# FFN 2 of a hybrid encoder block: two plain feature tiles of gate and up become an eleventh seven-product unit

## The chip, the cores and the metric

One core of one Trainium2 chip runs the whole kernel. The metric is the device time of one execution in microseconds (us), the median of several runs. Engines are named as in the profile: PE (matrix products), PEld (its weight loads), DVE (vector engine), ACT (scalar engine), POOL, and SP, which here issues most transfers. Each engine works off its own queue in the order in which the built program stands, and waits there for what another engine has to deliver.

## What is computed

The reference is one encoder layer on 512 tokens of width 1024: a half-step feed-forward (FFN 1), a mixing block (recurrent branch and attention, joined by a product with W_out), and a second half-step feed-forward (FFN 2). The change is in FFN 2:

```
def _rmsnorm(x, g):
    y = xf * lax.rsqrt(jnp.mean(xf * xf, axis=-1, keepdims=True) + EPS)
    return (y * g.astype(jnp.float32)).astype(x.dtype)

def _swiglu(h, w_gu, w_down):
    g, u = jnp.split(h @ w_gu, 2, axis=-1)
    return (jax.nn.silu(g) * u) @ w_down

x = x + (sigmoid(gA)*A + sigmoid(gB)*B) @ W_out
x = x + 1/2 * SwiGLU_2(RMSNorm(x))
```

D_FF is 2816, so gate and up have 22 feature tiles of 128 each.

## The kernel before, in words

Activations are held transposed: a tile has 128 features on the partitions and all 512 tokens along the row. Every product of float32 numbers is made of three products of rounded halves: an operand is cut into a high part (xh, wh; cast by ACT, L138) and a low part (xl, wl; the rest, subtracted by DVE, L141), and the PE adds high by high, high by low and low by high (`mm3`, L164).

**The step ahead of FFN 2** is the product with W_out (L988 to L1000). For each of 8 output tiles m the PE does 24 matmuls; then DVE adds the residual (L994), ACT makes xh (L187), a square (L196) and a scaled copy xg (L541), and DVE makes xl (L188) and adds the square to `ssum` (L197). From m = 4 on, `Forms.tile` makes four sums and differences of quarters of x ("forms" s1, s2, s4, s3, L238 to L264) for the pair (m - 4, m); `cut` splits them into high and low (L266), two pairs at a time, behind m = 5 and behind m = 7.

**A plain feature tile** (L417 to L428) takes two chunks, gate and up, of 24 matmuls of 512 tokens each (`feat_chunk`, L169; the weights come through `load_w`, L152). FFN 2 has `NPLAIN[1]` = 2 of these in front. Behind the first chunk stands `rstd` (L201): the PE transposes `ssum` (L211), DVE sums it (L212), ACT takes the root, DVE the reciprocal, the PE transposes it back (L219), and ACT writes the row of 1/rms that scales gate and up afterwards.

**A unit of seven products** (`strassen`, L273) makes two feature tiles of gate and of up at once by a Strassen-like scheme: gate and up on one side, the two halves of the tokens on the other, the inner dimension in two halves. Each `product` (L279) is 24 matmuls of 256 tokens. Per unit four blocks of 512 KB of weights are loaded: `a_` and `b_` into the buffers `wraw` (3 of them), `d` and `c` into buffers `pair` (4, which also hold the residual tiles). Four times two blocks are added on DVE (`after_sum`, L324, done at L323), and seven operands are split (`operand`, L292), into buffers wh and wl, of which there are 4 each: the eighth split waits until the fourth product is done, and so on. In the first unit the products are, in the order of the code, a11 on the operand `a_`, a12 on `c` (`gate1`, L333), then s1, s2, s4 and s3 on sums or on `b_`; the seventh (a22) is done inside the next unit. a11 uses xh and xl of the tiles 0 to 3, a12 of the tiles 4 to 7. The second product's result is scaled by 1/rms in `gate` (L298).

**What sets the order.** No order is written out: the framework's scheduler puts each engine's instructions in a row when the program is built. Splits of weights and sums of blocks are marked `tc.high_priority()` (L160, L294, L325), so the scheduler places them as early as it can.

Of the kernel before, what the change touches and what calls it, by code (L numbers as in the profile page):

```python
# [9 lines left out]
F32 = mybir.dt.float32  # L10
# [6 lines left out]
P = 128  # L17
T = 512
D = 1024
KT = D // P  # L20
DFF = 2816
FT = DFF // P
# [20 lines left out]
NLEAD = 6  # L43


NPLAIN = 4, 2

DTAIL = 3

# [2 lines left out]
AHEAD = 4  # L52
# [32 lines left out]
def block_kernel(ctx: ExitStack, tc, a, out):  # L85
# [3 lines left out]
    xpool = ctx.enter_context(tc.tile_pool(name="xpool", bufs=1))  # L89
# [11 lines left out]
    def nm(s):  # L101
        uid[0] += 1
        return f"{s}_{uid[0]}"
# [12 lines left out]
    def aux_t():  # L116
        return aux.tile([P, T], F32, tag="aux", name=nm("aux"))
# [4 lines left out]
    xd = dram.tile([KT, P, T], F32, name="xd")  # L122
# [75 lines left out]

        return xh, xl, ssum, one, square

    def rstd(ssum, lead=False):  # L201

        pc = aux_t()
        vx = tiny.tile([P, NCB], F32, tag="vx", name=nm("vx"))
        if lead:
            for j in range(NCB):
                nc.tensor.matmul(pc[:, j : j + 1], ssum[:, j * P : (j + 1) * P], ones[:, 0:1], start=True, stop=True)
            nc.vector.tensor_scalar(vx, pc[:, 0:NCB], 1.0 / D, EPS, ALU.mult, ALU.add)
        else:
            for j in range(NCB):  # L210
                nc.tensor.transpose(pc[:, j * P : (j + 1) * P], ssum[:, j * P : (j + 1) * P], ident)  # L211
            nc.vector.reduce_sum(vx, pc.rearrange("p (j f) -> p j f", j=NCB), axis=AX.X)  # L212
            nc.vector.tensor_scalar(vx, vx, 1.0 / D, EPS, ALU.mult, ALU.add)
        rcol = tiny.tile([P, NCB], F32, tag="rcol", name=nm("rcol"))
        nc.scalar.activation(rcol, vx, AF.Sqrt)
        nc.vector.reciprocal(rcol, rcol)
        ps = aux_t()
        for j in range(NCB):
            nc.tensor.transpose(ps[:, j * P : (j + 1) * P], rcol[:, j : j + 1].to_broadcast([P, P]), ident)  # L219
        r = xpool.tile([P, T], F32, tag="rstd", name=nm("rstd"))  # L220
        nc.scalar.activation(r, ps, AF.Copy)
        return r, rcol, vx

# [46 lines left out]

        return S, raw, cut

    def strassen(src, units, A, r, hs, ahead):  # L273

        half = T // 2
        prev = {}
        view = lambda t: t.rearrange("p (m t) -> p m t", m=2)

        def product(ps, w, form, first, last):  # L279
            H, L = w  # L280
            for m in range(2):
                o = ps[:, m * half : (m + 1) * half]
                for k in range(4):
                    c = slice((m * 4 + k) * P, (m * 4 + k + 1) * P)
                    xh_, xl_ = A[form][k]


                    for w_, x_ in ((H, xh_), (H, xl_), (L, xh_)):
                        nc.tensor.matmul(o, w_[:, c], x_, start=first and m + k == 0 and w_ is H and x_ is xh_,  # L289
                                         stop=m + k == 4 and w_ is L, skip_group_check=True)  # L290

        def operand(raw):  # L292
            w = hl_t()
            with tc.high_priority():  # L294
                split(raw, *w)
            return w

        def gate(t, tok):  # L298
            rr = r[:, tok].unsqueeze(1).to_broadcast([P, 2, half])
            s_ = big_t(n="s")  # L300
            nc.vector.tensor_tensor(view(s_), view(t), rr, ALU.mult)
            nc.scalar.activation(s_, s_, AF.Silu)
            return s_

        def put(u, s_, t, tok):
            for m in range(2):
                c = slice(m * half, (m + 1) * half)
                mark["h"] = nc.vector.tensor_tensor(hs[u * 2 + m][:, tok], s_[:, c], t[:, c], ALU.mult)

        def last_product(p):  # L310
            product(p["Z"], p["w"](), "a22", False, True)
            put(p["u"], gate(p["Z"], slice(half, T)), p["u7"], slice(half, T))

        for u in range(units):
            a_, b_ = raw_t(), raw_t()
            d = pair_t().rearrange("p a b -> p (a b)")
            c = pair_t().rearrange("p a b -> p (a b)")

            for t, i in ((a_, 0), (d, 1), (b_, 3), (c, 2)):
                nc.sync.dma_start(t, src[u, i])  # L320

            def add(t, o, i):
                nc.vector.tensor_tensor(t, t, o, ALU.add)  # L323
            def after_sum(t, o, i, add=add):  # L324
                with tc.high_priority():  # L325
                    add(t, o, i)
                return operand(t)

            Z, X, Y = acc_t(), acc_t(), aux_t()
            hs += [big_t(n="h") for _ in range(2)]  # L330
            last = u == units - 1

            def gate1():  # L333
                product(Y, w_c, "a12", True, True)
                nc.vector.tensor_tensor(p1, p1, Y, ALU.add)
                return gate(p1, slice(0, half))

            product(Z, operand(a_), "a11", True, False)
            p1 = big_t(n="p1")
            nc.scalar.activation(p1, Z, AF.Copy)  # L340
            w_c = operand(c)
            if not last:
                s1 = gate1()
            product(X, after_sum(a_, d, 1), "s1", True, False)
            p5 = big_t(n="p5")
            nc.scalar.activation(p5, X, AF.Copy)
            if prev:
                last_product(prev)
            product(Z, after_sum(a_, b_, 3), "s2", False, False)
            u2 = big_t(n="u2")  # L350
            nc.scalar.activation(u2, Z, AF.Copy)
            product(X, operand(b_), "s4", False, True)
            nc.vector.tensor_tensor(u2, u2, X, ALU.add)
            product(Z, after_sum(b_, d, 1), "s3", False, False)
            nc.vector.tensor_tensor(p5, p5, Z, ALU.add)
            if last:
                ahead()
                s1 = gate1()
            put(len(hs) // 2 - 1, s1, u2, slice(0, half))
            prev = dict(u=len(hs) // 2 - 1, Z=Z, u7=p5, w=lambda a_=a_, c=c, f=after_sum: f(a_, c, 2))  # L360
        last_product(prev)

    def ffn(wgu, ws, wd, xh, xl, S, ssum, plain, res, emit_out, lead=None, end=None):
        hs = []
        r = None
        pre = {}
        if lead is not None:
# [5 lines left out]
            for k in range(KT):  # L373
                lead[0](k)
                if k in LEAD_W:
                    n = LEAD_W[k]
                    o = (k % 4) * P
# [19 lines left out]
                w = [wts[i][k // 4] for i in range(NLEAD)]  # L397
                lead[2](k)
                if k == KT - 1:
                    r = rstd(ssum, True)[0]  # L400
# [16 lines left out]
        for m in range(plain):  # L417
            pg = chunk(2 * m)
            if r is None:
                r = rstd(ssum)[0]  # L420
            pu = chunk(2 * m + 1)
            g = big_t(n="g")
# [8 lines left out]
        A = {"a11": quarter(0, slice(0, half)), "a12": quarter(4, slice(0, half)),  # L431
             "a22": quarter(4, slice(half, T)), **S}
# [5 lines left out]
        def ahead(n):  # L438
            while len(cuts) < min(n, len(order)):
                qk = order[len(cuts)]  # L440
                cuts[qk] = big_t(F32R, n="hh"), big_t(F32R, n="hl")
                split(hs[qk[1]], *cuts[qk])

        strassen(ws, (FT - plain) // 2, A, r, hs, lambda: ahead(AHEAD))
        for q in range(2):
            outs = range(q * 4, q * 4 + 4)
            for i in range(2):
# [36 lines left out]
        i, x, k0 = 3, xres[KT - 1], FT - EHALF  # L484
        for k in range(FT - 2 * DTAIL, k0):
            put_in(i, k, k0 - 1)
        t, o, p2 = big_t(n="dn"), big_t(n="o"), aux_t()[:, :half]
# [40 lines left out]
    xh, xl, ssum, one, square = make_xg(C_G1, "a")  # L528
# [32 lines left out]
    forms = Forms(C_G1)  # L561
# [10 lines left out]
    def out1(m, ps):  # L572
# [6 lines left out]

    ffn(a["w1gu"], a["w1s"], a["w1d"], xh, xl, forms.S, ssum, NPLAIN[0], lambda m: a["x"][m], out1,  # L580
        (lead, one, lead_step, lambda: (forms.finish(), forms.finish())))
    xh, xl, ssum = nxt["v"][:3]
# [152 lines left out]
    A = [None] * KT  # L735
# [225 lines left out]
    for w, fn, scale in ((0, AF.Gelu_apprx_tanh, 1.0), (1, AF.Tanh, 0.5)):  # L961
        for fs in (range(0, 4), range(4, 8)):
            for f, t in gates(w, fs, fn, scale):
                until("lru", lambda: A[f] is not None)
                if w == 0:
                    o = big_t(n="A")
# [20 lines left out]
    forms = Forms(C_G2)  # L987
# [13 lines left out]
    xh, xl, ssum = nxt["v"][:3]  # L1001


    def out2(m, ps):
# [1 line left out]
        nc.vector.tensor_tensor(o, ps, xres[m], ALU.add)  # L1006
        nc.sync.dma_start(out[m], o)

    ffn(a["w2gu"], a["w2s"], a["w2d"], xh, xl, forms.S, ssum, NPLAIN[1], lambda m: xd[m], out2,
        end=lambda tok, o: nc.sync.dma_start(out[KT - 1][:, tok], o[:, tok]))  # L1010


def layouts(inp):

    f = lambda n: np.asarray(inp[n])
    con = np.ascontiguousarray
    o = {}
# [7 lines left out]
    for i in (1, 2):  # L1025
        w = f(f"w_ffn{i}_gu")[0]
        g, u = feat(w[:, :DFF]), feat(w[:, DFF:])
        n = NPLAIN[i - 1]
        o[f"w{i}gu"] = con(np.stack([g, u], 1)[:n]).reshape(2 * n, P, D)

        b = np.stack([g, u], 0)[:, n:].reshape(2, (FT - n) // 2, 2, P, 2, D // 2)
        o[f"w{i}s"] = con(b.transpose(1, 4, 0, 3, 2, 5)).reshape((FT - n) // 2, 4, P, D)
        d = f(f"w_ffn{i}_down")[0].reshape(FT // 2, 2, P, 2, T)
        o[f"w{i}d"] = con(d.transpose(3, 0, 2, 1, 4)).reshape(2, FT // 2, P, 2 * T)
    w = f("w_in")[0].reshape(D, 7, D)
# [49 lines left out]
```

## Time and profile before

| what | value |
|---|---|
| median of 3 runs | 1127.6 us (1127.58 to 1127.77) |
| the profiled execution, its own time | 1127.92 us |
| its span, first to last instruction | 1125.7 us |
| PE busy | 1114.5 us (99%) |
| PEld busy | 983.4 us (87%) |
| DVE busy | 834.9 us (74%) |
| ACT busy | 592.9 us (53%) |
| POOL busy | 52.3 us (5%) |
| chain of work that ended last | PE 96%, DVE 2%, issue 1%, ACT 1% |
| granted TensorE clock | 1.00 |

The span is the time from the first to the last instruction on the core; the execution's own time has 2.2 us more around it. Matmuls overlap in the pipeline, so the duration that the profile gives for one is longer than the distance from one start to the next; the distance is what counts for a sum. In the chain the lengths are these distances already added up.

### The profile page before, as it was taken

The numbers are of one execution on the slowest core, as the hardware profiler recorded it, in microseconds if no ns is written. First come the engines' busy times: TensorE is split into PE (matmuls) and PEld (weight loads), VectorE is DVE, ScalarE is ACT, GpSimd is POOL, SyncE is SP. The second block draws the span as 40 slices with busy tenths as digits, with TensorE's granted clock in tenths as the row PEclk, the third lists the DMA queues.
The fourth block names the chain that finished last, engine by engine and source line by source line (L and its number), as shares of the span: only waits on it lengthen the run. The fifth ranks groups of instructions, "written<-read, shape, count | busy, mean of one in ns | idle before, by whom it ended". The sixth has DMA issues, their size and how long they took to land.

```text
span 1125.7 us, 17414 instructions
## 1 busy us (share of the span) xinstructions
PE 1114.5 (99%) x6867; PEld 983.4 (87%) x6867; DVE 834.9 (74%) x1294; ACT 592.9 (53%) x897; POOL 52.3 (5%) x116
## 2 busy tenths in 40 slices
PE   9999999999999999999999999999999999999998
PEld 8899999988888777777888888888999999998887
DVE  7888888893736865899655877659688888894552
ACT  8554554563533668687464445446445445464330
POOL 0000000000000341120110000000000000000000
PEclk9999999999999999999999999999999999999999
DMA  7242333443423686573443342355134233252421
GB/s 265 93 127 80 114 112 95 132 134 98 143 80 103 164 231 174 151 193 94 135 147 103 94 124 64 105 180 183 57 95 118 90 112 114 94 169 94 131 75 38
DMA packets 46770, 138.04 MB, mean 123 GB/s; under 512 B 7008, under 2 KB 10592, under 8 KB 46688
## 3 DMA queue, kind: packets, MB, share of 16 engines
q1 hardware_dynamic: 39744, 118.31, 33.8%
q0 software_dynamic: 6368, 18.36, 5.9%
q8 instruction: 54, 0.88, 0.3%
q10 hardware_dynamic: 576, 0.26, 0.1%
q14 instruction: 28, 0.23, 0.1%
HBM read 120.12 MB, written 8.39 MB: 114 GB/s over the span
## 4 chain that ended last, share of the span: by engine, by line
PE 96%; DVE 2%; issue 1%; ACT 1%; DVEq 0%; ACTq 0%
PE acc L289 29%; PE acc L165 11%; PE acc L166 11%; PE acc L167 11%; PE aux L289 5%; PE aux L167 4%; PE aux L165 4%; PE aux L166 4%; PE acc L761 3%; PE acc L763 3%; PE acc L762 3%; PE aux L883 1%; PE aux L895 1%; PE aux L675 1%; PE aux L854 1%
## 5 line engine op out<-in xcount | busy, mean ns | idle before, releaser
L138 ACT ACTIVATE wh<-wraw 128x1024 fp32r<-128x1024 f32 (+3 forms) x242 | 239.8, 993 | 327.5 <-PE acc L289 95.9
L141 DVE TENSOR_TENSOR wl<-wraw,wh 128x1024 fp32r<-128x1024 f32 (+3 forms) x254 | 289.5, 1142 | 143.4 <-ACT wh L138 140.1
L289 PE MATMUL acc<-s,wh 128*128 128x256 f32 x1216 | 220.5, 283 | 0.0
L289 PEld LDWEIGHTS acc<-s,wh 128*128 128x128 f32 x1216 | 189.7, 192 | 0.0
L289 PE MATMUL acc<-s,wl 128*128 128x256 f32 x608 | 172.1, 283 | 0.0
L165 PE MATMUL acc<-xh,wh 128*128 128x512 f32 x304 | 120.4, 396 | 0.0
L167 PE MATMUL acc<-xh,wl 128*128 128x512 f32 x304 | 118.9, 391 | 0.0
L166 PE MATMUL acc<-xl,wh 128*128 128x512 f32 x304 | 118.8, 391 | 0.0
L289 PEld LDWEIGHTS acc<-s,wl 128*128 128x128 f32 x608 | 116.8, 192 | 0.0
L289 PE MATMUL acc<-xh,wl 128*128 128x256 f32 x304 | 86.0, 283 | 0.0
L289 PE MATMUL acc<-xl,wh 128*128 128x256 f32 x304 | 86.0, 283 | 0.0
L289 PE MATMUL acc<-xh,wh 128*128 128x256 f32 x304 | 86.0, 283 | 0.0
L761 PE MATMUL acc<-wh,xh 128*128 128x512 f32 x192 | 75.8, 396 | 1.9 <-DVE v L785 1.4
L762 PE MATMUL acc<-wh,xl 128*128 128x512 f32 x192 | 75.1, 391 | 0.0
L763 PE MATMUL acc<-wl,xh 128*128 128x512 f32 x192 | 75.0, 391 | 0.0
L323 DVE TENSOR_TENSOR wraw<-wraw,pair 128x1024 f32<-128x1024 f32 x57 | 69.5, 1220 | 0.8
L165 PE MATMUL aux<-hh,wh 128*128 128x512 f32 (+1 forms) x181 | 69.9, 386 | 0.0
L166 PE MATMUL aux<-hl,wh 128*128 128x512 f32 (+1 forms) x181 | 69.9, 386 | 0.0
L167 PE MATMUL aux<-hh,wl 128*128 128x512 f32 (+1 forms) x181 | 69.9, 386 | 0.0
L167 PE MATMUL acc<-hh,wl 128*128 128x512 f32 (+1 forms) x176 | 67.9, 386 | 0.0
L166 PE MATMUL acc<-hl,wh 128*128 128x512 f32 (+1 forms) x176 | 67.9, 386 | 0.0
L165 PE MATMUL acc<-hh,wh 128*128 128x512 f32 (+1 forms) x176 | 67.9, 386 | 0.0
(212 smaller groups left out, 2206.8 us busy)
## 6 DMA issues: line engine op xcount, KB each, us to landing
wraw<-wqkv SPq DMA_DIRECT2D x24, 512.0 KB, 4.5
wraw<-wg SPq DMA_DIRECT2D x24, 512.0 KB, 3.6
wraw<-w1d SPq DMA_DIRECT2D x22, 512.0 KB, 3.6
wraw<-w2d SPq DMA_DIRECT2D x22, 512.0 KB, 3.6
pair<-w2s SPq DMA_DIRECT2D x20, 512.0 KB, 3.6
wraw<-w2s SPq DMA_DIRECT2D x20, 512.0 KB, 3.6
wraw<-w1s SPq DMA_DIRECT2D x18, 512.0 KB, 3.6
pair<-w1s SPq DMA_DIRECT2D x18, 512.0 KB, 3.7
```

Source lines behind the costliest of these rows:

```text
L138: nc.scalar.activation(H, raw, AF.Copy)
L141: nc.vector.tensor_tensor(L, raw, H.bitcast(F32), ALU.subtract)
L165: nc.tensor.matmul(ps, wh, xh, start=first, stop=False, skip_group_check=skip)
L166: nc.tensor.matmul(ps, wh, xl, start=False, stop=False, skip_group_check=skip)
L167: mark["mm"] = nc.tensor.matmul(ps, wl, xh, start=False, stop=last, skip_group_check=skip)
L289: nc.tensor.matmul(o, w_[:, c], x_, start=first and m + k == 0 and w_ is H and x_ is xh_, stop=m + k == 4 and w_ is L, skip_group_check=True)
L323: nc.vector.tensor_tensor(t, t, o, ALU.add)
L675: prev, mm = mm, nc.tensor.matmul(ps[d][b], W[w][o, c], X[x][o], start=x == 1, stop=w + x == 0)
L761: nc.tensor.matmul(pss[j], xh[kk][:, tj], H[:, s], start=kk == 0, stop=False)
L762: nc.tensor.matmul(pss[j], xl[kk][:, tj], H[:, s], start=False, stop=False)
L763: mark["mm"] = nc.tensor.matmul(pss[j], xh[kk][:, tj], L[:, s], start=False, stop=kk == KT - 1)
L854: mm = hold(nc.tensor.matmul(ps[hp][:, i * 256 : (i + 1) * 256], q_[o, n * P : (n + 1) * P], keys(k_[o]), start=k_ is kl, stop=q_ is ql))
```

## The change

FFN 2 has no plain tile: `NPLAIN` is `4, 0`, so all 22 feature tiles go through 11 units instead of 2 plain tiles and 10 units. As `rstd` stood behind the first plain chunk, it is now called inside the first unit, behind its second product (a12), and writes into a tile that is allocated ahead of the units. The weights of the two tiles move from the array of plain chunks to that of the units; their bytes stay the same.

```diff
-NPLAIN = 4, 2
+NPLAIN = 4, 0
...
-    def rstd(ssum, lead=False):
+    def rstd(ssum, lead=False, r=None):
...
-        r = xpool.tile([P, T], F32, tag="rstd", name=nm("rstd"))
+        if r is None:
+            r = xpool.tile([P, T], F32, tag="rstd", name=nm("rstd"))
...
-    def strassen(src, units, A, r, hs, ahead):
+    def strassen(src, units, A, r, hs, ahead, late=None):
...
             def gate1():
                 product(Y, w_c, "a12", True, True)
+                if u == 0 and late is not None:
+                    late()
                 nc.vector.tensor_tensor(p1, p1, Y, ALU.add)
                 return gate(p1, slice(0, half))
...
-        strassen(ws, (FT - plain) // 2, A, r, hs, lambda: ahead(AHEAD))
+        if r is None:
+            r = xpool.tile([P, T], F32, tag="rstd", name=nm("rstd"))
+            late = lambda: rstd(ssum, False, r)
+        else:
+            late = None
+        strassen(ws, (FT - plain) // 2, A, r, hs, lambda: ahead(AHEAD), late)
...
-    ffn(a["w2gu"], a["w2s"], a["w2d"], xh, xl, forms.S, ssum, NPLAIN[1], lambda m: xd[m], out2,
+    ffn(None, a["w2s"], a["w2d"], xh, xl, forms.S, ssum, NPLAIN[1], lambda m: xd[m], out2,
```

The order of the instructions changes only from the end of the W_out product on. In the rows below a tile's name is followed by its numbers.

**DVE, behind the last W_out tile (m = 7).** Here `acc_1414` is that tile's result, `xl_1359` the low part of x tile 7, `ssum_1360` the sum of squares. Before:

```order
L242 TENSOR_TENSOR s1_1410_7711<-xg_1409_7709,xg_1373_7517 128x256
L240 SCALAR_TENSOR_TENSOR s2_1411_7713<-s1_1410_7711,xg_1373_7517 128x256
L240 SCALAR_TENSOR_TENSOR s4_1412_7715<-s2_1411_7713,xg_1409_7709 128x256
L242 TENSOR_TENSOR s3_1413_7717<-xg_1373_7517 128x256
L994 SCALAR_TENSOR_TENSOR pair_1339_7380<-acc_1414_7720,pair_1339_7380 128x512
L141 TENSOR_TENSOR wl_1451_7900<-wraw_1449_7898,wh_1450_7899 128x1024
L188 SCALAR_TENSOR_TENSOR xl_1359_7428<-pair_1339_7380,small_78,xh_1358_7427 128x512
L197 TENSOR_TENSOR ssum_1360_7429<-ssum_1360_7429,xsq_1418_7754 128x512
```

And in the change, where `wraw_1429` holds a_ and the sums made of it, `wraw_1430` b_, `pair_1432` c and `pair_1431` d of the first unit:

```order
L243 TENSOR_TENSOR s1_1410_7711<-xg_1409_7709,xg_1373_7517 128x256
L1002 SCALAR_TENSOR_TENSOR pair_1339_7380<-acc_1414_7720,pair_1339_7380 128x512
L141 TENSOR_TENSOR wl_1452_7906<-wraw_1429_7781,wh_1451_7905 128x1024
L241 SCALAR_TENSOR_TENSOR s2_1411_7713<-s1_1410_7711,xg_1373_7517 128x256
L324 TENSOR_TENSOR wraw_1429_7781<-wraw_1429_7781,pair_1432_7784 128x1024
L141 TENSOR_TENSOR wl_1455_7936<-wraw_1430_7782,wh_1454_7935 128x1024
L241 SCALAR_TENSOR_TENSOR s4_1412_7715<-s2_1411_7713,xg_1409_7709 128x256
L324 TENSOR_TENSOR wraw_1430_7782<-wraw_1430_7782,pair_1431_7783 128x1024
L243 TENSOR_TENSOR s3_1413_7717<-xg_1373_7517 128x256
L188 SCALAR_TENSOR_TENSOR xl_1359_7428<-pair_1339_7380,small_78,xh_1358_7427 128x512
L197 TENSOR_TENSOR ssum_1360_7429<-ssum_1360_7429,xsq_1418_7754 128x512
```

Between the residual add of m = 7 and its xl stood one split of weights; now there are two splits, two sums of blocks and three forms.

**PE, where xl of x tile 7 is first used.** Before, it is the last k of the first plain chunk (`acc_1428`), with the transposes of `ssum` behind it:

```order
L165 MATMUL acc_1428_7780<-xh_1356_7425,wh_1430_7782 128x512
L166 MATMUL acc_1428_7780<-xl_1357_7426,wh_1430_7782 128x512
L167 MATMUL acc_1428_7780<-xh_1356_7425,wl_1431_7783 128x512
L165 MATMUL acc_1428_7780<-xh_1358_7427,wh_1430_7782 128x512
L166 MATMUL acc_1428_7780<-xl_1359_7428,wh_1430_7782 128x512
L167 MATMUL acc_1428_7780<-xh_1358_7427,wl_1431_7783 128x512
L211 MATMUL aux_1432_7811<-ident_83,ssum_1360_7429 128x128 x4
```

In the change it is inside the second product of the first unit (a12, `aux_1435`), of which ten matmuls stand ahead of these six of s1 (`acc_1434`), and fourteen from the xl row on:

```order
L290 MATMUL aux_1435_7791<-xh_1358_7427,wh_1441_7824 128x256
L290 MATMUL acc_1434_7790<-s1_1396_7654,wh_1448_7874 128x256
L290 MATMUL acc_1434_7790<-s1_1397_7655,wh_1448_7874 128x256
L290 MATMUL acc_1434_7790<-s1_1396_7654,wl_1449_7875 128x256
L290 MATMUL acc_1434_7790<-s1_1396_7654,wh_1448_7874 128x256
L290 MATMUL acc_1434_7790<-s1_1397_7655,wh_1448_7874 128x256
L290 MATMUL acc_1434_7790<-s1_1396_7654,wl_1449_7875 128x256
L290 MATMUL aux_1435_7791<-xl_1359_7428,wh_1441_7824 128x256
L290 MATMUL aux_1435_7791<-xh_1358_7427,wl_1442_7825 128x256
```

The first use of xl of tile 7 moved from the 23rd matmul of 512 tokens behind W_out to the 41st of 256; the transposes of `ssum` and the 18 other matmuls of s1 follow behind a12.

**PE, behind the product s1 of the first unit.** Before, s2 of the same unit (`acc_1459`) follows s1:

```order
L289 MATMUL acc_1460_7943<-s1_1420_7764,wh_1470_8010 128x256
L289 MATMUL acc_1460_7943<-s1_1421_7765,wh_1470_8010 128x256
L289 MATMUL acc_1460_7943<-s1_1420_7764,wl_1471_8011 128x256
L289 MATMUL acc_1459_7942<-s2_1398_7658,wh_1473_8041 128x256
L289 MATMUL acc_1459_7942<-s2_1399_7659,wh_1473_8041 128x256
```

In the change, seven matmuls of a11 of the second unit (`acc_1462`, with its split operand `wh_1467` and `wl_1468`) stand between s1 and s2 (`acc_1433`):

```order
L290 MATMUL acc_1434_7790<-s1_1420_7764,wl_1449_7875 128x256
L290 MATMUL acc_1462_8004<-xh_1344_7413,wh_1467_8009 128x256
L290 MATMUL acc_1462_8004<-xl_1345_7414,wh_1467_8009 128x256
L290 MATMUL acc_1462_8004<-xh_1344_7413,wl_1468_8010 128x256
L290 MATMUL acc_1462_8004<-xh_1346_7415,wh_1467_8009 128x256
L290 MATMUL acc_1462_8004<-xl_1347_7416,wh_1467_8009 128x256
L290 MATMUL acc_1462_8004<-xh_1346_7415,wl_1468_8010 128x256
L290 MATMUL acc_1462_8004<-xh_1348_7417,wh_1467_8009 128x256
L290 MATMUL acc_1433_7789<-s2_1398_7658,wh_1451_7905 128x256
```

The splits go through the four buffers in the order a_, c, s1, s2, s4, s3 of the first unit and then a_ of the second, so `wh_1467` takes the buffer of `wh_1448`, the operand of s1.

## Rows read from the trace of the kernel before

**Rows 1.** The page, busy time, share of the span and count by engine.

```profile
PE 1114.5 (99%) x6867; PEld 983.4 (87%) x6867; DVE 834.9 (74%) x1294; ACT 592.9 (53%) x897; POOL 52.3 (5%) x116
```

**Rows 2.** PE's longest wait in the span: total us, times, longest us.

```profile
PE acc L761 <- DVE v L785: 1.4, 1, 1.4
```

**Rows 3.** PE's order of time, W_out's end and the units' start: start, us.

```profile
777.61 0.39 PE L167 MATMUL acc<-yh,wl 128*128 128x512 f32 x1
777.84 0.39 PE L165 MATMUL acc<-xh,wh 128*128 128x512 f32 x1
...
800.54 0.28 PE L289 MATMUL acc<-xh,wh 128*128 128x256 f32 x1
800.66 0.28 PE L289 MATMUL acc<-xl,wh 128*128 128x256 f32 x1
```

**Rows 4.** The chain that ended last, same place: start, us, what.

```profile
783.45 0.44 PE aux L211 x4
...
790.49 0.44 PE aux L219 x4
...
820.86 2.88 PE aux L289 x24
...
841.02 2.88 PE aux L289 x24
```

**Rows 5.** Windows, units 3 to 10: us, then busy by engine, PEclk, DMA.

```profile
842.00:1005.00 163.00, 163.00 (x1349) 162.51 (x1349) 140.83 (x166) 84.72 (x105) 0.00 (x0) 1.00 0.38 117
```

**Rows 6.** DVE in order of time: start, us, instruction [idle before <- releaser].

```profile
761.72 0.69 DVE L994 SCALAR_TENSOR_TENSOR pair<-acc,pair 128x512 f32<-128x512 f32 x1 [2.08 <-PE acc L167]
...
768.07 1.23 DVE L141 TENSOR_TENSOR wl<-wraw,wh 128x1024 fp32r<-128x1024 f32 x1 [0.23 <-ACT wh L138]
...
777.14 0.41 DVE L242 TENSOR_TENSOR s<-xg,xg 128x256 f32<-128x256 f32 x1
777.59 0.88 DVE L240 SCALAR_TENSOR_TENSOR s<-s,xg 128x256 f32<-128x256 f32 x2
...
778.73 0.68 DVE L994 SCALAR_TENSOR_TENSOR pair<-acc,pair 128x512 f32<-128x512 f32 x1
779.33 1.21 DVE L141 TENSOR_TENSOR wl<-wraw,wh 128x1024 fp32r<-128x1024 f32 x1
780.46 0.75 DVE L188 SCALAR_TENSOR_TENSOR xl<-pair,small,xh 128x512 fp32r<-128x512 f32 x1
781.12 0.68 DVE L197 TENSOR_TENSOR ssum<-ssum,xsq 128x512 f32<-128x512 f32 x1
781.73 0.42 DVE L242 TENSOR_TENSOR s<-xg,xg 128x256 f32<-128x256 f32 x1
782.06 0.42 DVE L242 TENSOR_TENSOR s<-xg 128x256 f32<-128x256 f32 x1
...
786.72 1.22 DVE L323 TENSOR_TENSOR wraw<-wraw,pair 128x1024 f32<-128x1024 f32 x1
787.86 0.68 DVE L141 TENSOR_TENSOR s<-s,s 128x512 fp32r<-128x512 f32 x1
```

**Rows 7.** ACT and DVE in order of time: the split of a unit's operand.

```profile
800.57 1.06 ACT L138 ACTIVATE wh<-wraw 128x1024 fp32r<-128x1024 f32 x1 [3.85 <-PE acc L166]
...
801.66 1.23 DVE L141 TENSOR_TENSOR wl<-wraw,wh 128x1024 fp32r<-128x1024 f32 x1 [0.16 <-ACT wh L138]
```

**Rows 8.** SP in order of time: when block c of the first unit is issued.

```profile
759.14 0.33 SPq L320 DMA_DIRECT2D pair<-w2s  x1
```

**Rows 9.** Issues by line, 735 to 810 us: count, KB, median us to landing.

```profile
pair<-w2s SPq DMA_DIRECT2D x6, 512.0 KB, 4.3
```

**Rows 10.** PE in order of time, the kernel's first microseconds.

```profile
1.06 3.78 PE L131 MATMUL aux<-ones 128*128 128x128 f32 x16 [1.06 <-DVE pol L600]
4.69 1.65 PE L402 MATMUL acc<-xh,wh 128*128 128x512 f32 x3
6.13 0.93 PE L402 MATMUL aux<-xh,wh 128*128 128x512 f32 x3
```

More of the change, by code (lines that the diff above doesn't have):

```diff
@@ L1028, in layouts @@
         n = NPLAIN[i - 1]
-        o[f"w{i}gu"] = con(np.stack([g, u], 1)[:n]).reshape(2 * n, P, D)
+        if n:
+            o[f"w{i}gu"] = con(np.stack([g, u], 1)[:n]).reshape(2 * n, P, D)
         b = np.stack([g, u], 0)[:, n:].reshape(2, (FT - n) // 2, 2, P, 2, D // 2)
```

## Prediction, made before the changed kernel ran

> **What bounds the kernel now.** I read the page first: PE is busy for 99% of the span [rows 1], so time is saved by taking matmuls away and lost wherever PE is made to wait. Then the list of PE's waits: the longest single one is 1.4 us, in the attention part [rows 2], and none lies in FFN 2. Then the chain and PE's order of time at the place of the change. W_out's last matmul starts at 777.61 and the first plain chunk's at 777.84, with no gap; the first unit begins at 800.54 [rows 3]. From there the chain is PE alone, unit behind unit: the same product, a12, of units 2 and 3 stands at 820.86 and 841.02 [rows 4], so a unit takes 20.16 us, 0.120 us for each of its 168 matmuls. Last I read DVE at W_out's end, since DVE feeds PE there. It waits for W_out's result of m = 4 at 761.72, having idled 2.08 us, but adds the residual of m = 7 only at 778.73 [rows 6], some 0.7 us after that result could be had (three chunks of 5.44 us later than 761.72 is 778.04). So DVE is already a little late before the change, and what is put in its queue there counts.
>
> **Matmuls.** Removed: four chunks of 24 matmuls of 512. The stretch 777.84 to 800.54 is 22.70 us and holds them and two groups of transposes of 0.44 us [rows 3, 4], so they take 21.82 us, 0.227 each. Added: one unit, 20.16 us. The transposes stay. Saving: **1.7 us**. The Trainium skill, page "TensorE: Matmul & The Clock Gate", section "Wait — 56ns, not 53.3ns?", puts the distance of matmuls at columns over 2.4 GHz plus about 2.5 ns; by that, 96 of 512 less 168 of 256 would save 2.4 us, an estimate. The rows have 13 ns over the columns' own time in both sizes, and they decide.
>
> **DVE at W_out's end, first stall.** Between the residual add of m = 4 and xl of m = 7, DVE's queue before holds four splits of weights; in the change it holds five, and all four sums of the first unit's blocks; the forms and cuts ahead of that xl are as many as before. A split's subtract holds DVE for 1.13 us (779.33 to 780.46), a sum for 1.14 (786.72 to 787.86) [rows 6]. Added: 4 x 1.14 + 1.13 = 5.7 us. Some of it fills gaps: 0.23 us ahead of the subtract at 768.07, about as much ahead of the residual of m = 5, and 0.12 in front of each form that needs the one just made (777.14 to 777.59 is 0.45, where independent forms stand 0.33 apart, 781.73 to 782.06) [rows 6]; with four of the latter, 0.9 us. So xl of m = 7 starts not at 780.46 but 4.8 us later, at **785.2**, and is there at 786.0 (0.75 us) [rows 6]. The bounds are 786.2, if no gap is filled, and about 784.2, if twice as much is; I take the middle, because the gaps are rows.
>
> PE meanwhile runs a11 from 777.84, 24 x 0.12 = 2.9 us, ten matmuls of a12 (1.2) and the six of s1 that stand ahead of the xl row (0.7), and is at that row at 782.65. It waits until 786.0: **3.3 us** lost (2.4 to 4.3 by the bounds). Before, the same row stood 22 x 0.227 = 5.0 us behind 777.84, at 782.8, and xl was there at 781.2.
>
> **Second stall.** The rest of a12 (14), the transposes and the 18 other matmuls of s1 take 1.7 + 0.4 + 2.2 = 4.3 us, to 790.3. The squares' sum follows xl on DVE by 0.7 us [rows 6], in time for the transposes. Then come the seven matmuls of the second unit's a11. Their operand takes the buffer of s1's, so its cast can't start before s1's last matmul is through. What such a split costs from the moment that PE releases it: ACT casts for 1.06 us from 800.57, and DVE's subtract starts 0.03 us after that and lasts 1.23 [rows 7]. PE waits some 1.2 us for the cast (matmul's end included), does two matmuls, 0.24 us, and waits for the subtract for another 1.0 us: **2.2 us** lost. It is 1.2 at least, when the subtract is hidden somehow. Who waits for PE here is s2, whose operands have long been there; it follows undisturbed.
>
> **1/rms and the transfers.** `rstd`'s own work is the same, in another place. Behind xl, at 785.9, DVE has `ssum`, five forms and two cuts ahead of its reduction (0.60 or 0.33 each [rows 6], to 789.1), then the reduction, two splits, two cuts and a sum ahead of the small scaling; as the second of these splits ends only at 792.7 (above), that scaling comes at about 794.4, and root and reciprocal, tiny ones, at about 795.2. PE has been held until 792.75, does five more matmuls of a11, all of s2 and one more, and is at the transposes of L219 at 796.4. So 1/rms is covered by 1.2 us; without that cover PE would wait for it, and then `gate`, which is needed only for h. The two table loads of ACT stand in both orders. On SP the first unit's blocks take the places of the plain chunks; c, the latest of them, is issued as before at 759.14 [rows 8], takes some 4.3 us [rows 9], and is cast at about 767. Nothing else waits on SP there. In the later units DVE is busy for 140.8 of 163 us and PE for all of it [rows 5]; one more such unit brings no wait.
>
> **Sum.** -1.7 + 3.3 + 2.2 = **+3.8 us**. The profiled execution would go from 1127.9 to 1131.7; the median shown is 0.3 us lower, so I forecast **1131.4**.
>
> **Rivals.** A measurement of this kernel can tell about 0.2%, 2.3 us, from no change: same is 1125.3 to 1129.9.
>
> *xl is in time* (not slower). If xl of m = 7 starts by 781.9, the first stall is gone, and what is left is -1.7 + 2.2: 1128.1. It decides at DVE's queue between 779 and 785: two sums, two splits and three forms would have to be done by W_out's end. Against it: the splits wait for PE (the one of b_ until a11 is done, as it takes that buffer), and DVE is late already [rows 6]. 7%.
>
> *Neither stall*, the plain reading of the change as a saving of matmuls: 1125.9. For it speaks that PE never waits in the ten units of before [rows 5]; against it, that each of those starts with its operands made long ahead. 5%.
>
> *The clock falls behind the first stall* (slower still). No row of before has PE idle for over 1.4 us [rows 2], and the granted clock is 1.00 throughout, so what 3.3 us do is not shown. The nearest rows are the kernel's start: 16 warm-up matmuls take 3.78 us, the first ones of 512 stand some 0.6 us apart and the next group under 0.3 [rows 10]; some of that is waiting for weights. Were all of 1.06 to 6.13 at the 1.2 GHz level, that costs half of 5.1 us, so 2.5 us here too: 1133.9. The Trainium skill, same page, section "HAM oscillation — how this bites in real kernels", has idle gaps of PE throw the clock back to half, so that the next work starts cold; no run here shows that so far. 13%.
>
> *The lateness lasts*, another microsecond or more where the second unit's first operands are made, because DVE is behind with everything: 1133 to 1136. 7%.
>
> **The numbers.** The forecast has 68%: by the bounds of its two stalls (2.4 + 1.2 to 4.3 + 2.2) it lies between 1129.5 and 1132.4. With the clock's case the range goes to 1134.0; below, 1129.4 leaves out xl in time and no stall. Left out are some 14 to 18%. Slower: 68 + 13 + 7 = 88%, less 1 for the lower edge of the forecast; same: 7 + 5 - 1 + 1 = 12%; faster: 1%, if the whole saving is had and a little more.
>
> **What would show it.** In the new profile: PE's waits have two new entries of over 1 us, one for xl on DVE (about 3.3 us, at some 786) and one for the cast and the subtract of a split at some 790 to 793; xl of m = 7 starts near 785.2 on DVE; all units behind that run at 20.16 us without a gap; the granted clock stays 1.00. The prediction is wrong if PE runs through a12 without a wait, if a wait of over 1 us stands at L219 or in a later unit, or if matmuls behind the stall stand 0.24 us apart.

## The result, and the profile after

The changed kernel took 1132.47 us in the median of five runs (1132.33 to 1133.38), the kernel before 1127.69 us on the same chip (1127.58 to 1127.88): ratio 1.0044, interval 1.0030 to 1.0057, so slower by 4.8 us where 3.8 were forecast. The profiled execution took 1133.38 us (span 1131.2) at a mean granted clock of 0.998; the four others took 1132.33 to 1132.80 at 1.000. Run again on another chip (experiment e9_change_again, below) it had a median of 1133.72 us. Where that spread comes from is a part of the explanation.

The page of the changed kernel, busy time by engine, against [rows 1]; PE has 72 matmuls more, 168 of 256 for 96 of 512:

```profile
PE 1114.8 (99%) x6939; PEld 986.5 (87%) x6939; DVE 843.5 (75%) x1306; ACT 598.1 (53%) x903; POOL 52.2 (5%) x116
```

Its list of PE's waits (total us, times, longest us), the three entries that the list of before does not have; there the longest was 1.4 us [rows 2]:

```profile
PE aux L290 <- DVE xl L188: 3.3, 1, 3.3
...
PE acc L290 <- ACT wh L138: 1.1, 1, 1.1
...
PE acc L290 <- DVE wl L141: 0.8, 1, 0.8
```

DVE of the changed kernel in order of time, from the residual add of m = 4 and then from that of m = 7 on, against [rows 6]:

```profile
761.30 0.69 DVE L1002 SCALAR_TENSOR_TENSOR pair<-acc,pair 128x512 f32<-128x512 f32 x1 [2.08 <-PE acc L167]
...
764.02 1.22 DVE L324 TENSOR_TENSOR wraw<-wraw,pair 128x1024 f32<-128x1024 f32 x1
...
778.68 0.68 DVE L1002 SCALAR_TENSOR_TENSOR pair<-acc,pair 128x512 f32<-128x512 f32 x1
779.28 1.21 DVE L141 TENSOR_TENSOR wl<-wraw,wh 128x1024 fp32r<-128x1024 f32 x1
780.41 0.41 DVE L241 SCALAR_TENSOR_TENSOR s<-s,xg 128x256 f32<-128x256 f32 x1
780.75 1.22 DVE L324 TENSOR_TENSOR wraw<-wraw,pair 128x1024 f32<-128x1024 f32 x1
781.88 1.22 DVE L141 TENSOR_TENSOR wl<-wraw,wh 128x1024 fp32r<-128x1024 f32 x1
783.02 0.41 DVE L241 SCALAR_TENSOR_TENSOR s<-s,xg 128x256 f32<-128x256 f32 x1
783.35 1.22 DVE L324 TENSOR_TENSOR wraw<-wraw,pair 128x1024 f32<-128x1024 f32 x1
784.49 0.41 DVE L243 TENSOR_TENSOR s<-xg 128x256 f32<-128x256 f32 x1
784.83 0.74 DVE L188 SCALAR_TENSOR_TENSOR xl<-pair,small,xh 128x512 fp32r<-128x512 f32 x1
...
792.73 1.23 DVE L141 TENSOR_TENSOR wl<-wraw,wh 128x1024 fp32r<-128x1024 f32 x1 [0.74 <-ACT wh L138]
...
796.28 0.17 DVE L216 RECIPROCAL rcol<-rcol 128x4 f32<-128x4 f32 x1
```

DVE never idles from 778.68 to 785.6: two splits, two sums and three forms stand between the residual and xl, which starts 6.15 us behind the residual add instead of 1.73. On DVE the order changes earlier than "from the end of the W_out product on", as it is told above: the first sum of blocks stands at 764.02, behind xl of m = 4, and a second one at 775.34. PE's own order does change only there. PE of the changed kernel in order of time:

```profile
777.19 0.39 PE L167 MATMUL acc<-yh,wl 128*128 128x512 f32 x1
...
782.09 0.28 PE L290 MATMUL acc<-s,wl 128*128 128x256 f32 x1
785.62 0.42 PE L290 MATMUL aux<-xl,wh 128*128 128x256 f32 x1 [3.25 <-DVE xl L188]
785.84 0.41 PE L290 MATMUL aux<-xh,wl 128*128 128x256 f32 x1
...
788.62 0.91 PE L211 MATMUL aux<-ident,ssum 128*128 128x128 f32 x4
789.28 0.49 PE L290 MATMUL acc<-s,wh 128*128 128x256 f32 x2
...
791.39 0.28 PE L290 MATMUL acc<-s,wl 128*128 128x256 f32 x1
792.75 0.38 PE L290 MATMUL acc<-xh,wh 128*128 128x256 f32 x1 [1.08 <-ACT wh L138]
792.97 0.28 PE L290 MATMUL acc<-xl,wh 128*128 128x256 f32 x1
794.01 0.39 PE L290 MATMUL acc<-xh,wl 128*128 128x256 f32 x1 [0.76 <-DVE wl L141]
794.23 0.28 PE L290 MATMUL acc<-xh,wh 128*128 128x256 f32 x1
...
797.70 0.60 PE L219 MATMUL aux<-ident,rcol 128*128 128x128 f32 x4
```

Two things are to be seen. Both stalls stand at the forecast places, and L219 waits for nothing (the reciprocal was done at 796.45). And the 14 matmuls from 785.62 to 788.62 stand 0.214 us apart instead of 0.120. The windows of the changed kernel (us, busy by engine, granted clock PEclk, DMA share, GB/s) say why:

```profile
778.00:786.00 8.00, 4.75 (x39) 4.55 (x38) 8.00 (x12) 3.42 (x5) 0.00 (x0) 0.99 0.38 109
786.00:790.00 4.00, 4.00 (x24) 4.00 (x23) 3.24 (x8) 2.56 (x4) 0.00 (x0) 0.59 0.66 241
790.00:794.00 4.00, 2.17 (x17) 1.76 (x15) 3.26 (x5) 2.62 (x5) 0.00 (x0) 1.00 0.35 126
842.00:1005.00 163.00, 163.00 (x1361) 163.00 (x1360) 139.83 (x163) 82.62 (x100) 0.00 (x0) 1.00 0.37 111
```

Behind the 3.25 us in which PE stood still, the granted clock was at the 1.2 GHz level (0.59 is the mean with the stretch behind the transposes, which has 2.4 GHz again). 256 columns at 1.2 GHz are 0.213 us. Units 3 to 10 of before ran with PE never idle [rows 5], and so do those of the change. The chain of waits has the same product, a12, of two successive units 20.16 us apart, as before [rows 4]:

```profile
826.30 2.88 PE aux L290 x24
...
846.46 2.88 PE aux L290 x24
```

### The profile page after: what moved, and what is told of

It reads as the page before. It is cut to its first block, busy times and chain, and to the rows that moved or that the text cites. A ratio compares the mean times of both kernels' runs of the same rounds, so it can differ in the third digit from the quotient of the medians.

```text
span 1131.2 us, 17575 instructions
## 1 busy us (share of the span) xinstructions
PE 1114.8 (99%) x6939; PEld 986.5 (87%) x6939; DVE 843.5 (75%) x1306; ACT 598.1 (53%) x903; POOL 52.2 (5%) x116
## 4 chain that ended last, share of the span: by engine, by line
PE 93%; DVE 4%; issue 2%; ACT 1%; DVEq 0%; ACTq 0%
PE acc L290 30%; PE acc L165 10%; PE acc L166 10%; PE acc L167 10%; PE aux L290 5%; PE aux L165 4%; PE aux L166 4%; PE aux L167 4%; PE acc L769 3%; PE acc L771 3%; PE acc L770 3%; PE aux L891 1%; PE aux L903 1%; PE aux L683 1%; DVE wl L141 1%
## 5 line engine op out<-in xcount | busy, mean ns | idle before, releaser
L290 PE MATMUL acc<-s,wh 128*128 128x256 f32 x1280 | 232.4, 283 | 0.0
L290 PEld LDWEIGHTS acc<-s,wh 128*128 128x128 f32 x1280 | 199.6, 192 | 0.1
L290 PE MATMUL acc<-s,wl 128*128 128x256 f32 x640 | 181.1, 283 | 0.0
L290 PEld LDWEIGHTS acc<-s,wl 128*128 128x128 f32 x640 | 122.9, 192 | 0.0
L165 PE MATMUL acc<-xh,wh 128*128 128x512 f32 x272 | 107.8, 396 | 0.0
L166 PE MATMUL acc<-xl,wh 128*128 128x512 f32 x272 | 106.3, 391 | 0.0
L167 PE MATMUL acc<-xh,wl 128*128 128x512 f32 x272 | 106.3, 391 | 0.0
L290 PE MATMUL acc<-xh,wh 128*128 128x256 f32 x320 | 90.6, 283 | 1.1 <-ACT wh L138 1.1
L290 PE MATMUL acc<-xh,wl 128*128 128x256 f32 x320 | 90.7, 284 | 0.8 <-DVE wl L141 0.8
L290 PE MATMUL acc<-xl,wh 128*128 128x256 f32 x320 | 90.5, 283 | 0.0
```

Of the source, the lines that this page charges most:

```text
L165: nc.tensor.matmul(ps, wh, xh, start=first, stop=False, skip_group_check=skip)
L166: nc.tensor.matmul(ps, wh, xl, start=False, stop=False, skip_group_check=skip)
L167: mark["mm"] = nc.tensor.matmul(ps, wl, xh, start=False, stop=last, skip_group_check=skip)
```

## The experiments

Ratios are against runs of the kernel before on the same chip. One account serves all of them: from W_out's last matmul to 830 us I add up what PE's starts are further apart than 0.120 us (matmuls of 256), 0.227 (of 512) and 0.065 (transposes), idle matmuls of an experiment counted with them. Before, that excess is 0.39 us. Excess less 0.39, less the 1.63 that a unit is shorter than four chunks, should be the difference of the profiled execution from the kernel before. For e1, which has two plain tiles more and a unit less, the 1.63 is added.

| kernel | excess, us | by the account | its profiled execution, less before's median | median of all its runs, less before's |
|---|---|---|---|---|
| the change | 7.88 | +5.9 | +5.7 | +4.8 |
| e1_four_plain | 0.36 | +1.6 | +2.1 | +1.9 |
| e2_hold_clock | 4.84 + 3.12 idle matmuls | +5.9 | +5.9 | +5.6 |
| e3_plain_priority | 4.38 | +2.4 | +2.2 | +2.3 |
| e4_ordered | 1.63 | -0.4 | -0.3 | -0.4 |
| e5_fill_both | 1.44 + 5.04 idle matmuls | +4.5 | +4.2 | +4.5 |
| e6_xl_first | 8.58 | +6.6 | +6.5 | +6.5 |
| e7_rms_behind_s3 | 8.68 | +6.7 | +6.8 | +6.3 |
| e8_second_unit_last | 11.96 | +9.9 | +10.1 | +8.9 |
| e9_change_again | 7.90 | +5.9 | +6.0 | +6.0 |
| e10_rms_behind_s3_again | 7.66 | +5.6 | +5.7 | +4.7 |

The account closes to 0.5 us everywhere, and to 0.3 in ten of eleven. What is left is for the most part where W_out's last matmul stands in the execution (777.19 in the change, 778.05 in e1, 777.61 before): with that added, it meets the difference of the profiled spans (1125.7 before) to 0.03 us in all eleven. So what follows can be read from PE's gaps between 777 and 830 us alone.

**What is a unit worth against two plain tiles?** Two tiles more are made plain, the other way round from the change:

```diff
-NPLAIN = 4, 0
+NPLAIN = 4, 4
...
-    ffn(None, a["w2s"], a["w2d"], ...
+    ffn(a["w2gu"], a["w2s"], a["w2d"], ...
```

> The kernel before with four plain tiles in front of FFN 2 and nine units: the same swap in the other direction, with 1/rms behind the first plain chunk. If the forecast's price of the swap is right (21.8 us of plain chunks against 20.16 us of a unit), it is 1.6 to 1.7 us slower than before, 1129.3 us, and PE waits nowhere in FFN 2. If units are dearer than counted (the loss of the change is the price of a unit itself), it is faster than before, by up to 4.8 us.

1129.72 us against 1127.84, ratio 1.0016 (1.0007 to 1.0025), eleven runs: +1.9 us (0.8 to 2.8), PE without a wait in FFN 2. The matmul term is confirmed, for the swap in the other direction: a unit is cheaper, and the change loses all of that and more at its waits.

**Does the idle time throw the clock?** 26 matmuls into a bank that nobody reads keep PE busy ahead of the late xl row:

```diff
+                        if late is not None and form == "a12" and not filled and m == 0 and k == 3 and x_ is xl_:
+                            filled.append(aux_t())
+                            for _ in range(26):
+                                d_ = nc.tensor.matmul(filled[0][:, :half], H[:, :P], A[form][0][0], start=True, stop=True)
...
```

> The change, with 26 idle matmuls of 256 tokens put on PE in front of the row that waits for xl of x tile 7; they fill 3.1 of the 3.3 us of waiting and are thrown away, so nothing else moves. If the clock's fall behind the wait costs what the profile of the change shows (14 matmuls 0.214 apart where 0.120 is usual, and the transposes behind them: some 1.5 us), the time falls by the mean of that over the runs, 0.9 us, to 1131.5 us, which is before plus the two waits less the saving (3.8 us), and matmuls behind the wait stand 0.120 apart. If the clock costs nothing, it stays at 1132.5 us; if the dummies are in the way, it is slower than the change.

1133.45 us, ratio 1.0048 (1.0036 to 1.0061): no gain, a miss. Four of its five executions had a mean clock of 0.998; the one at 1.000 took 1132.50 us. PE of this kernel in order of time:

```profile
781.76 3.28 PE L294 MATMUL aux<-xh,wh 128*128 128x256 f32 x26
...
785.89 0.39 PE L300 MATMUL aux<-xl,wh 128*128 128x256 f32 x1
786.12 0.28 PE L300 MATMUL aux<-xh,wl 128*128 128x256 f32 x1
786.23 0.28 PE L300 MATMUL aux<-xh,wh 128*128 128x256 f32 x1
...
792.86 0.39 PE L300 MATMUL acc<-xh,wl 128*128 128x256 f32 x1 [0.76 <-DVE wl L141]
...
793.56 0.59 PE L300 MATMUL acc<-s,wh 128*128 128x256 f32 x2
793.96 0.41 PE L300 MATMUL acc<-s,wl 128*128 128x256 f32 x1
794.17 0.63 PE L300 MATMUL acc<-s,wh 128*128 128x256 f32 x2
```

Behind the xl row the matmuls stand 0.12 apart: the clock held there. But it fell behind the second stall instead; from 793.56 to 796.7 the matmuls of s2 stand 0.21 apart. My theory had allowed only for the long wait. So the same idle matmuls were put into the two shorter waits too, 9 and 7 of them:

> The change, with idle matmuls on PE in all its waits: 26 ahead of the row that needs xl of x tile 7, 9 ahead of the second unit's first matmul and 7 ahead of its third (the one that needs the low part). If the rest that the change and the run with the first wait filled show over the forecast (+4.8 and +5.6 us against +3.8) is the clock, which falls behind whichever wait is left open, every run now has the clock at 1.000, matmuls stand 0.120 apart throughout, and the time is before + 3.8 to 4.0 us, 1131.7 us. If it stays at 1132.5 us or more with the clock up, there is a cost besides waits and clock.

1132.25 us, ratio 1.0039 (1.0026 to 1.0051), five runs within 0.5 us. The windows of this kernel:

```profile
786.00:790.00 4.00, 4.00 (x35) 3.97 (x34) 3.97 (x9) 2.73 (x4) 0.00 (x0) 1.00 0.67 243
790.00:794.00 4.00, 3.99 (x32) 3.66 (x31) 3.85 (x5) 3.35 (x4) 0.00 (x0) 1.00 0.47 135
794.00:800.00 6.00, 6.00 (x53) 6.00 (x52) 3.00 (x7) 3.38 (x6) 0.00 (x0) 1.00 0.01 1
```

With PE never idle the clock stays at 2.4 GHz (0.999 or 1.000 in the mean of all five executions), and the rest of the loss stays too. This is the change without the clock's part: the two stalls, their restarts and the shorter matmuls, +4.5 us.

**What makes xl late?** In the first unit the sums a + b, b + d and a + c with their splits, and the split of b itself, lose their priority; all else is as in the change:

```diff
-        def operand(raw):
+        def operand(raw, tag=None):
             w = hl_t()
+            if late is not None and tag in ((True, 3, True), (True, 1, False), (True, 2, True), (True, 's4')):
+                split(raw, *w)
+                return w
...
+                if late is not None and tag in ((True, 3, True), (True, 1, False), (True, 2, True)):
+                    add(t, o, i)
+                    return operand(t, tag)
...
```

> The change, with the first unit's later weights (the sums a+b, b+d and a+c and the splits of these and of b) at the scheduler's usual priority; the arithmetic is the same. Order theory: these stood ahead of xl of x tile 7 in DVE's queue and made the first wait. With xl at about 782 the wait of 3.3 us is gone, the clock stays up, and there remain waits of at most 1 us each, together 3.2 us (cut of s1, the transposes of 1/rms, the second unit's first operands): before + 1.6 us, 1129.3 us. If DVE simply had too much to do at that place, another wait of 3 us or more stands in its stead, and it stays at 1132 us.

1130.09 us, ratio 1.0020 (1.0011 to 1.0029), at a mean clock of 1.0 in all eleven runs. The 3.25 us wait is gone (0.14 us of excess are left at that row), so what made xl late is the work that was placed ahead of it. It missed the expected time by 0.8 us. Shorter waits of 3.2 us in all had been allowed for; five came (0.72 for a cut form, 0.36 for the reciprocal at L219, and 0.49, 0.45 and 0.31 behind that), and from start to start, with what PE takes to restart behind each, PE lost 4.0 us more than before.

A second way is to let xl go first: the call that makes xh and xl of x tile m is put at high priority from m = 4 on, the square and `ssum` are not:

```diff
-        nxt["v"][3](m)
+        if m >= KT // 2:
+            with tc.high_priority():
+                nxt["v"][3](m)
+        else:
+            nxt["v"][3](m)
```

> The change, with xh and xl of the x tiles 4 to 7 at high priority, nothing else. If xl alone were the trouble, the first wait goes and the time falls by 3.4 us or more, to 1129 us. By the order theory the sums and splits still stand there, now ahead of the sum of squares: PE waits some 3.8 us at the transposes of it (L211) in place of xl, 1.3 us more at s1's cut, and less at the second unit's operands; before + 4.6 us and the clock's part, 1132.5 to 1133.5 us, no gain.

1134.30 us, ratio 1.0057 (1.0041 to 1.0072). PE of this kernel in order of time:

```profile
784.02 0.28 PE L290 MATMUL acc<-s,wl 128*128 128x256 f32 x1
788.16 1.09 PE L211 MATMUL aux<-ident,ssum 128*128 128x128 f32 x4 [3.86 <-DVE ssum L197]
...
790.31 0.41 PE L290 MATMUL acc<-s,wl 128*128 128x256 f32 x1
790.52 0.63 PE L290 MATMUL acc<-s,wh 128*128 128x256 f32 x2
```

The xl row is passed in time, and PE stops a few matmuls later, at the transposes of `ssum`, for 3.86 us: `ssum` stands behind sums, splits and forms on DVE and starts at 787.33. The wait that I had expected there came, and with it the clock's fall until about 794.5, which I had not priced fully.

**The place of 1/rms, and of the second unit.** In e7 `rstd` and the scaling stand behind s3; in e8 the second unit's a11 is held behind the product before it:

```diff
                 product(Y, w_c, "a12", True, True)
+                return None if u == 0 and late is not None else gate2()
+
+            def gate2():
                 if u == 0 and late is not None:
...
```

> The change, with 1/rms and the scaling that needs it made behind the first unit's product s3, three products later. If making 1/rms behind a12 is what costs, this is faster by the part that it had. By the forecast it is covered there, and the two waits stand at the same places with the same lengths (3.3 us for xl, 1.2 and 1.0 us for the second unit's operand): the same time as the change, 1132.5 us.

```diff
+                        if behind is not None:
+                            after(i_, behind)
+                            behind = None
+            mark["pr"] = i_
...
-            product(Z, operand(a_), "a11", True, False)
+            product(Z, operand(a_), "a11", True, False, mark["pr"] if u == 1 and late is not None else None)
```

> The change, with the second unit's a11 held behind all products of the first unit on PE. If the second wait is due to those seven matmuls standing early, it goes and 2.2 us are saved: 1130 us. If they stand there because PE would wait anyway (s2 writes into the result of a11, which ACT has to have copied, and that copy stands in ACT's queue behind casts that wait for PE and DVE), s2 waits some 2.2 us instead and the second unit's a12 another 1.8 us: slower, before + 5.8 us, 1133.6 us.

e7 took 1134.08 us, ratio 1.0056 (1.0042 to 1.0070), with the change's three waits (3.3, 1.1, 0.8). e8 took 1136.68 us, ratio 1.0078 (1.0065 to 1.0092). Its first new wait, on PE and then what ACT did meanwhile:

```profile
795.08 0.79 PE L290 MATMUL acc<-s,wh 128*128 128x256 f32 x2 [2.08 <-ACT p L347]
```

```profile
792.97 1.06 ACT L138 ACTIVATE wh<-wraw 128x1024 fp32r<-128x1024 f32 x1 [2.12 <-issue]
793.93 0.61 ACT L138 ACTIVATE s<-s 128x512 fp32r<-128x512 f32 x1
794.45 0.58 ACT L347 ACTIVATE p<-acc 128x512 f32<-128x512 f32 x1
```

Without the seven hoisted matmuls s2 waits 2.08 us for the copy of a11's result (L347 there, L343 in the change), which frees the bank that s2 writes and stands behind two casts on ACT; and the two waits of the second unit's split (0.64 and 0.75) come all the same at 800 us. So the hoisting did not cost the second stall; it covered another one. Both runs were longer than their waits explain, at mean clocks of 0.995 to 0.998. In e7's profile the clock stays low for longer behind the same wait: PE's distances are those of 1.2 GHz (0.214 us for 256 columns) to 791.6, in the change's profile to 789.2. Its windows:

```profile
786.00:790.00 4.00, 3.91 (x18) 3.91 (x19) 3.28 (x8) 1.93 (x3) 0.00 (x0) 0.50 0.81 259
790.00:794.00 4.00, 3.11 (x20) 2.90 (x18) 2.42 (x3) 1.83 (x3) 0.00 (x0) 0.79 0.09 33
```

To see whether e7's 1.6 us over the change were the place of 1/rms or the clock, both ran once more on one chip:

> The changed kernel itself, unaltered, beside the next one on one chip. Theory (the waits cost 3.4 + 2.2 us in every execution, and the clock's fall behind the first wait costs another 0 to 2 us that differs from execution to execution): the runs lie between 1132.0, what the kernel with idle matmuls in all waits took, and some 1134; those with a mean clock of 0.997 or 0.998 are 1 to 2 us longer than those with 1.000. Rival (the 1131.2 us span of the first profile is a single disturbance): all runs lie within 0.4 us of 1132.4, at a mean clock of 1.000.

> The kernel with 1/rms and the scaling behind the product s3 in the first unit, once more, now on the same chip as the change. Theory (its waits are the change's; what it took more, 1.6 us in the medians, was the clock, which stayed low for longer): its median is within 0.7 us of the change's on this chip, or, if longer, the runs that are longer have the lower mean clock, and the first wait and the two behind it are 3.3, 1.1 and 0.8 us again. Rival (the other place of 1/rms costs time of its own): slower than the change by 1.5 us at the same mean clock.

Now the change was the longer one: 1133.72 us, ratio 1.0056 (1.0042 to 1.0070), against 1132.37, ratio 1.0043 (1.0030 to 1.0056). The place of 1/rms costs nothing. The change's ten executions of both calls order themselves by their mean clock: five at 1.000 took 1132.2 to 1132.8 us, three at 0.998 took 1133.4 to 1133.7, two at 0.997 took 1135.0 and 1135.2. The waits in both of its profiles are the same to 0.01 us. So the clock alone, by its mean, tells the short executions from the long ones; the two at 0.997 were not profiled.

**A version with an order.** e3, and besides: `rstd` and scaling as in e7, the second unit's a11 as in e8, and the casts of three splits (s3, a22, the second unit's first) held behind ACT's copy of the result of s1:

```diff
+            if late is not None and tag in ((True, 1, False), (True, 2, True), (1, 'a11')):
+                after(mark["H"], mark["p5"])
...
-            nc.scalar.activation(p5, X, AF.Copy)
+            i_ = nc.scalar.activation(p5, X, AF.Copy)
+            if u == 0 and late is not None:
+                mark["p5"] = i_
...
```

> As the run before, and three things more: 1/rms and the scaling by it behind the product s3, the second unit's a11 behind all of the first unit's products, and the casts for s3, a22 and the second unit behind the copy of s1's result. Order theory: both waits gone but for about 1 us at s1's cut, so the saving of the matmuls shows: -1.7 + 1.0 = 0.6 us faster than before, 1127.1 us. If the second wait is not one of order, it comes back somewhere, and the time is 1129 us or more.

1127.45 us, ratio 0.9996 (0.9987 to 1.0005): 0.4 us under the kernel before, from which it can't be told, where the change was 4.8 and 6.0 us over it. On DVE xl of m = 7 now starts 2.74 us behind its residual (779.08):

```profile
781.82 0.74 DVE L188 SCALAR_TENSOR_TENSOR xl<-pair,small,xh 128x512 fp32r<-128x512 f32 x1
```

PE of this kernel passes the xl row with hardly a gap, and has one wait in FFN 2, for a cut form:

```profile
782.25 0.40 PE L290 MATMUL acc<-s,wh 128*128 128x256 f32 x2
782.62 0.39 PE L290 MATMUL aux<-xl,wh 128*128 128x256 f32 x1
...
785.97 0.39 PE L290 MATMUL acc<-s,wh 128*128 128x256 f32 x1 [0.58 <-DVE s L141]
```

Of the 1.6 us that the matmuls save, 1.2 go to this wait and the restarts (1.63 less 0.39). Which of its three additions to e3 took away the waits that e3 still had was not tested apart.

## Why the prediction was right, and where it was off

**Direction and range** were right: slower, by 4.8 and 6.0 us in two sets of five, inside 1129.4 to 1134.0 in both medians; two of ten single executions, at 1135, lie outside. 1131.4 was too low by 1.1 and 2.3.

**Matmuls, -1.7 us**: right. 1.6 by PE's starts, 1.9 (0.8 to 2.8) by e1.

**First stall, 3.3 us**: right in size and place: 3.25 in the list, 3.41 from start to start beyond 0.12. xl was forecast at 785.2 on DVE; it started at 784.83 in an execution in which W_out's last matmul stands 0.42 us earlier (777.19 for 777.61 [rows 3]), so 785.25 on the scale of before. Of the 5.7 us of added work 0.9 filled gaps, as forecast: from the residual of m = 4 to xl of m = 7 are 23.53 us (761.30 to 784.83) where 18.74 were before, 4.8 more. e3 shows the cause: with the priority taken away from the sums and splits, the wait is gone.

**Second stall, 2.2 us**: right: 1.24 behind the cast and 0.92 behind the subtract, 2.16. But the hoisted matmuls are only half of it. The prediction lets s2, "whose operands have long been there", wait for nothing but PE; that leaves out the bank that s2 writes. e8 shows PE held in the same place for that bank, 2.08 us, if the second unit's matmuls stand elsewhere.

**1/rms covered by 1.2 us**: right. The reciprocal ended at 796.45 and L219 started at 797.70, and e10 shows that its place makes no difference. On the scale of before both came 1.7 us later than forecast, by the clock and the restarts below, so that the cover stayed the same.

**Later units unharmed, at 20.16 us**: right.

**"The granted clock stays 1.00"** is the step that failed, in some executions, and the prediction's own sign of it came: matmuls behind the stall, expected 0.24 us apart in that case, stand 0.214 apart. *The clock falls behind the first stall* was held at 13%, because no row of before has PE idle for over 1.4 us. It came in five of ten executions, to judge by their mean clock. Its price, forecast at 2.5 us, was 1.5 in the profiled one (13 distances between matmuls by 0.093, and 0.3 at the transposes over what they take before), some 2.3 in e7's profile (6.7 by the account, less 4.3, below) and about 2.7 in the two at 0.997 (1135.1 less 1132.4). e2 and e5 show what throws it: with all three waits filled the mean clock was 0.999 or 1.000 in five of five executions, with the first alone filled in one of five, with none in five of ten; these are few, but the profile of e2 shows the fall moved from the filled wait to the open ones. The Trainium skill, page "TensorE: Matmul & The Clock Gate", section "HAM oscillation — how this bites in real kernels", which has idle gaps of PE throw the clock back, was borne out by 0.214 us between matmuls behind the 3.25 us wait. I had weighed it too low.

**A term was missing.** The first matmul behind each wait stands 0.22 us ahead of the next, also at full clock (792.75 to 792.97, 794.01 to 794.23), so each restart costs 0.1 us: 0.3 for the three. With it the change at full clock is -1.6 + 3.4 + 2.2 + 0.3 = 4.3 us, and with the clock's 1.5 it is 5.8, for 5.9 by the account of the profiled execution. e5 has 4.5; the five executions at 1.000 have 4.7 (1132.4 less 1127.7). The last 0.4 are not placed; nine executions of the kernel before, beside e5, differ by 0.65 among themselves (1127.64 to 1128.29).

The rivals *xl is in time* and *neither stall* fell with the first wait; *the lateness lasts* fell with the units; 1135 was reached all the same, in two executions with a mean clock of 0.997.

## What to carry to other kernels

A saving of matmuls at a change of stage is only had if the operands of the first products are there, and "high priority" on weight preparation can put it, in an in-order queue, ahead of the one small operation that PE needs next: count what stands between that operation and its input on its own engine. A wait on PE of a few microseconds costs more than its length, since the clock may fall behind it, and the price then differs from execution to execution; judge such a version by several runs with their clocks. Where one wait is removed, ask which is behind it: moving xl forward alone, or the second unit back alone, turned one wait into another, and of the versions tried only the one that ordered the whole transition gave the time back.

## What the runs showed of the hardware that was not expected

The clock fell in e2 behind two waits of 1.08 and 0.76 us that end 1.3 us apart, though single waits of up to 1.4 us in the kernel before left it at 1.00 [rows 2]; and it fell 0.7 us after PE was at work again (matmuls 0.12 apart from 793.09 to 793.56, then 0.21). Behind the first wait, the same in all three, it stayed low for different times: PE's distances are those of 1.2 GHz from 785.6 to 789.2 us in the change, from 786.6 to 789.9 in its second profile (e9), and from 786.1 to 791.6 in e7. The same kernel with the same waits kept a mean clock of 1.000 in five executions and not in five others. What decides that was not found.
